# Six channel blocks summed by column additions instead of a strided reduction

## The chip, the cores and the metric

The kernel runs on one core of a Trainium2 chip. The metric is the device time of one execution in microseconds; before the change three timed runs gave 3150.18, 3155.59 and 3156.21 us, a median of 3155.59. Engines are named as the profile names them: PE is TensorE (matmuls), DVE is VectorE, ACT is ScalarE, POOL is GpSimd, SP is the queue that issues most DMAs. TensorE writes its results to the accumulator memory PSUM; the tiles that the other engines work on lie in SBUF, or are read from PSUM.

## The reference, cut to what matters

One layer of a decoder over a prompt of 2048 rows and 32 sample rows. Its input projection feeds three branches: windowed attention (A), a depthwise convolution with a LayerNorm over 768 channels (B), and cross-attention into 256 memory tokens (C). The change lies in the LayerNorm of branch B:

```
def _layernorm(x, g, b):
    x32 = x.astype(jnp.float32)
    mu = jnp.mean(x32, axis=-1, keepdims=True)
    var = jnp.mean(jnp.square(x32 - mu), axis=-1, keepdims=True)
    y = (x32 - mu) * lax.rsqrt(var + EPS)
    return (y * g.astype(jnp.float32) + b.astype(jnp.float32)).astype(x.dtype)
...
    ob = jax.nn.silu(_layernorm(conv, ln_g, ln_b))
```

## The kernel before, in words

The kernel has three large parts. The first (to about 870 us) projects the input onto q, k, v, the convolution's input and qc, and runs the convolution. The second runs the norm of branch B, the memory keys and values, the cross-attention, the sample attention and then the prompt's attention, and beside all of it a filler: the projections of the gates (tiles `gg`, function `sweep`), 7680 matmuls of 256 or 288 columns whose results ScalarE and VectorE evacuate (L243, L245, L246). The third (from about 2560 us) projects and merges the branches.

Nobody writes the order of the instructions by hand. The program is recorded, and a scheduler simulates it and fixes from its own costs and from priorities the order in which each engine's queue holds its instructions. On the chip each queue then runs strictly in that order. So TensorE has filler to do at nearly every moment, but a matmul of the norm that stands next in its queue stops it until its input is there.

The convolution's result is kept as six blocks of 128 channels by 2080 positions. `conv_norm` takes it in chunks of 256 positions (nine, the last of 32), as a tile `c` of 128 partitions by 6 blocks by 256 columns. For each chunk:

- a load brings `c` (L663); three such tiles are in use in turn;
- L665 sums the six blocks column by column into `sm`, with one `tensor_reduce` over a view in which the six values of a column are 256 elements apart;
- L667 multiplies by a matrix of ones, which sums over the partitions as well (result `str`), and L668 subtracts the mean from `c`;
- L671, on ScalarE, squares `c` into `sq`, of which there is one buffer; L673 sums its six blocks, again with a strided `tensor_reduce`; L675 is the matmul by ones (result `sco`);
- L677 makes the variance, then `rsqrt` (L63 on ScalarE, L64 to L68 on VectorE) its reciprocal root, and L679 scales `c`;
- L681, on GpSimd, applies gain and shift, one instruction a block; L684, on ScalarE, takes a tanh into the same `sq`, and L685 multiplies `c` by it. L686 stores it.

Because of the single `sq`, a chunk's square waits for L685 of the chunk before. `conv_norm` is a generator: `memory_kv` advances it by a chunk after each block of the memory projection, and `memory` runs what is left. GpSimd splits the weights meanwhile into a rounded part and a rest (L55, L56, tiles `whi` and `wlo`), for the filler and for the memory projection (matmuls `kv`).

Of the kernel before, what the change touches and what calls it, by code (L numbers as in the profile page):

```python
# [7 lines left out]
F32 = mybir.dt.float32  # L8
R32 = mybir.dt.float32r
AF = mybir.ActivationFunctionType  # L10
ALU = mybir.AluOpType
AX = mybir.AxisListType
# [25 lines left out]
class K:  # L38
# [616 lines left out]
    def conv_norm(self, lp, ps):  # L655
        nc = self.nc
        ones = lp.tile([128, 128], F32, name="ones")
        nc.vector.memset(ones, 1.0)
        W = 256
        for s in range(0, T, W):  # L660
            n = min(W, T - s)
            x = lp.tile([128, 6, W], F32, name="c", bufs=3)[:, :, :n]
            nc.sync.dma_start(x, self.d_c[:, :, s:s + n].rearrange("j p n -> p j n"))  # L663
            sm = lp.tile([128, W], F32, name="sm", bufs=2)[:, :n]
            nc.vector.tensor_reduce(sm, x.rearrange("p j n -> p n j"), axis=AX.X, op=ALU.add)  # L665
            p = ps.tile([128, 512], F32, name="str")[:, :n]
            nc.tensor.matmul(p, ones, sm, start=True, stop=True)  # L667
            nc.vector.scalar_tensor_tensor(x, p[:, None, :].to_broadcast([128, 6, n]), -1.0 / EB, x,  # L668
                                           op0=ALU.mult, op1=ALU.add)
            sq = lp.tile([128, 6, W], F32, name="sq", bufs=1)[:, :, :n]  # L670
            nc.scalar.activation(sq, x, AF.Square)  # L671
            sm = lp.tile([128, W], F32, name="sm", bufs=2)[:, :n]
            nc.vector.tensor_reduce(sm, sq.rearrange("p j n -> p n j"), axis=AX.X, op=ALU.add)  # L673
            p = ps.tile([128, 512], F32, name="sco")[:, :n]
            nc.tensor.matmul(p, ones, sm, start=True, stop=True)  # L675
            var = lp.tile([128, W], F32, name="var")[:, :n]
            nc.vector.tensor_scalar(var, p, 1.0 / EB, EPS, op0=ALU.mult, op1=ALU.add)  # L677
            rs = self.rsqrt(lp, var, [128, W], "ln", n)
            nc.vector.tensor_tensor(x, x, rs[:, None, :].to_broadcast([128, 6, n]), op=ALU.mult)  # L679
            for j in range(6):  # L680
                nc.gpsimd.tensor_scalar(x[:, j], x[:, j], self.v("ln_g", j), self.v("ln_b", j),  # L681
                                        op0=ALU.mult, op1=ALU.add)
            t = lp.tile([128, 6, W], F32, name="sq", bufs=1)[:, :, :n]
            nc.scalar.activation(t, x, AF.Tanh, scale=0.5)  # L684
            nc.vector.scalar_tensor_tensor(x, t, 1.0, x, op0=ALU.add, op1=ALU.mult)  # L685
            nc.sync.dma_start(self.d_actb[:, :, s:s + n].rearrange("j p n -> p j n"), x)  # L686
            yield
# [620 lines left out]
```

## Time and profile before

| | |
|---|---|
| Median of three timed runs | 3155.59 us |
| Profiled execution | 3154.4 us |
| Its span, first to last instruction | 3152.6 us |
| Busy in the span | PE 95%, DVE 64%, POOL 43%, ACT 36% |
| Mean granted TensorE clock | 0.979 of full speed |
| Chain that ended last | PE 70%, DMA 12%, DVE 7%, issue 4%, POOL 3%, ACT 2% |
| L665, all nine | 23.2 us of DVE |
| L673, all nine | 23.5 us of DVE |

A row of instructions reads: line, engine, operation, output<-inputs, shapes, count, then busy time. "Idle before" is how long the engine stood still in front of such instructions, and the name behind the arrow is what ended that. TensorE is busy for most of the span in every part, so the question for any stretch is how long it stands still there, and for whom.

### The profile page before, as it was taken

How to read it: one execution, taken by the hardware profiler on the slowest of the kernel's cores; microseconds unless marked ns; L12 is line 12 of the kernel's file. 1: busy time of each engine (PE TensorE's matmuls, PEld its weight loads, DVE VectorE, ACT ScalarE, POOL GpSimd, SP SyncE). 2: the span in 40 equal slices, each digit the busy share in tenths (PEclk: the TensorE clock that was granted, in tenths of full speed). 3: DMA queues.
4: the chain of work that ended last, by engine and by line, in shares of the span. 5: the costliest groups of instructions: out<-in, count | busy, mean ns of one | idle time of the engine just before them, and what ended most of it. 6: DMA issues, size and time to landing. Idle time of an engine off the chain costs nothing.

```text
span 3152.6 us, 55374 instructions
## 1 busy us (share of the span) xinstructions
PE 3000.2 (95%) x20705; PEld 2839.9 (90%) x20705; DVE 2014.8 (64%) x3734; ACT 1124.2 (36%) x2835; POOL 1350.4 (43%) x1048
## 2 busy tenths in 40 slices
PE   7999999999987999999999999989899979999998
PEld 6899999999987999998999999989898967787897
DVE  5297797796677926465546766666656457556563
ACT  5010010010132433243437575656565523222221
POOL 0121221142356537444256565667676433233240
PEclk9899999999999999999999999999999989999999
DMA  7232222211265454477454656576555487657561
GB/s 250 85 103 80 80 60 61 63 62 50 81 182 167 135 153 144 147 219 239 151 139 116 161 123 163 128 185 150 156 143 152 109 279 227 223 168 227 161 197 53
DMA packets 532218, 454.66 MB, mean 144 GB/s; under 512 B 118191, under 2 KB 458581, under 8 KB 531137
## 3 DMA queue, kind: packets, MB, share of 16 engines
q1 hardware_dynamic: 357502, 335.36, 36.2%
q10 hardware_dynamic: 169840, 105.02, 11.7%
q0 software_dynamic: 4608, 10.75, 1.2%
q8 instruction: 164, 2.69, 0.4%
q14 instruction: 104, 0.85, 0.1%
HBM read 332.96 MB, written 118.04 MB: 143 GB/s over the span
## 4 chain that ended last, share of the span: by engine, by line
PE 70%; DMA 12%; DVE 7%; issue 4%; POOL 3%; ACT 2%; SPq 1%; ACTq 0%; DVEq 0%; POOLq 0%
PE g L166 8%; PE g L167 8%; PE g L168 8%; PE gg L166 6%; PE gg L168 6%; PE gg L167 6%; PE pg L168 3%; PE pg L166 3%; PE pg L167 3%; PE pt L571 2%; DMA cb<-d_cf 2%; PE y L1180 2%; PE y L1179 2%; PE y L1178 2%; PE o L598 1%
## 5 line engine op out<-in xcount | busy, mean ns | idle before, releaser
L166 PE MATMUL gg<-x0h,whi 128*128 128x256 f32 (+1 forms) x2560 | 747.9, 292 | 25.9 <-DVE st L246 12.2
L168 PE MATMUL gg<-x0h,wlo 128*128 128x256 f32 (+1 forms) x2560 | 741.8, 290 | 0.1
L167 PE MATMUL gg<-x0l,whi 128*128 128x256 f32 (+1 forms) x2560 | 741.1, 290 | 0.0
L55 POOL TENSOR_SCALAR whi<-wraw 128x1024 fp32r<-128x1024 f32 x162 | 242.7, 1500 | 928.5 <-PE g L167 524.1
L166 PEld LDWEIGHTS gg<-x0h,whi 128*128 128x128 f32 x2560 | 493.2, 193 | 35.0 <-DVE st L246 13.7
L167 PEld LDWEIGHTS gg<-x0l,whi 128*128 128x128 f32 x2560 | 493.5, 193 | 2.2 <-issue 0.5
L168 PEld LDWEIGHTS gg<-x0h,wlo 128*128 128x128 f32 x2560 | 493.2, 193 | 2.2 <-POOL wlo L56 0.3
L322 DVE SCALAR_TENSOR_TENSOR acc<-G,cw,acc 128x1536 f32<-128x1536 f32 (+15 forms) x354 | 480.8, 1408 | 0.3
L56 POOL TENSOR_TENSOR wlo<-wraw,whi 128x1024 fp32r<-128x1024 f32 x162 | 417.0, 2575 | 9.4 <-PE gg L168 0.2
L155 POOL TENSOR_TENSOR clo<-craw,chi 128x768 fp32r<-128x768 f32 (+1 forms) x96 | 174.1, 1815 | 346.0 <-ACT chi L154 329.8
L627 ACT ACTIVATE P<-T,stm 128x128 f32<-128x128 f32 (+1 forms) x576 | 260.8, 455 | 141.0 <-DVE stm L625 94.8
L239 ACT ACTIVATE st<-g 128x384 f32<-128x384 f32 (+1 forms) x132 | 60.2, 461 | 570.7 <-PE g L168 550.7
L166 PE MATMUL pg<-ac,chi 128*128 128x512 f32 (+1 forms) x640 | 229.4, 359 | 16.6 <-ACT chi L154 8.7
L625 DVE CUSTOM_DVE_ANT_0 T<-s,bias 128x128 f32<-128x128 f32 (+1 forms) x576 | 191.5, 357 | 80.8 <-PE s L617 47.0
L167 PE MATMUL pg<-ac,chi 128*128 128x512 f32 (+1 forms) x640 | 228.8, 358 | 6.3 <-DVE ac L1198 6.3
L168 PE MATMUL pg<-ac,clo 128*128 128x512 f32 (+1 forms) x640 | 227.6, 357 | 3.6 <-POOL clo L155 3.6
L576 DVE TENSOR_TENSOR pl<-pt,ph 128x512 fp32r<-128x512 f32 x240 | 155.6, 652 | 52.4 <-ACT ph L575 48.9
L168 PE MATMUL g<-x0h,wlo 128*128 128x384 f32 x544 | 184.3, 339 | 2.9 <-POOL wlo L56 2.9
L166 PE MATMUL g<-x0h,whi 128*128 128x384 f32 x544 | 183.6, 338 | 2.6 <-ACT st L239 2.3
L167 PE MATMUL g<-x1l,whi 128*128 128x384 f32 x544 | 186.0, 342 | 0.0
L167 PE MATMUL g<-x0l,whi 128*128 128x384 f32 x544 | 185.8, 342 | 0.0
L168 PE MATMUL g<-x1h,wlo 128*128 128x384 f32 x544 | 185.8, 342 | 0.0
(330 smaller groups left out, 7425.0 us busy)
## 6 DMA issues: line engine op xcount, KB each, us to landing
wraw<-in_w_in ACTq DMA_DIRECT2D x119, 512.0 KB
d_g<-st ACTq DMA_DIRECT2D x168, 128.0 KB
cb<-d_cf SPq DMA_DIRECT2D x72, 256.0 KB
g<-d_g SPq DMA_DIRECT2D x72, 256.0 KB
wraw<-in_w_in SPq DMA_DIRECT2D x35, 512.0 KB
kvc<-in_cache_k_win SPq DMA_DIRECT2D x8, 1536.0 KB
kvc<-in_cache_v_win SPq DMA_DIRECT2D x8, 1536.0 KB
raw<-d_q SPq DMA_DIRECT2D x48, 256.0 KB
```

The costliest lines, as they stand in the source:

```text
L55: nc.gpsimd.tensor_scalar(hi, raw, 1.0, 1.0, op0=ALU.mult, op1=ALU.mult)
L56: nc.gpsimd.tensor_sub(lo, raw, hi.bitcast(F32))
L155: nc.gpsimd.tensor_sub(lo, raw, hi.bitcast(F32))
L166: nc.tensor.matmul(ps, hi[:, k, :], h, start=k == 0, stop=False)
L167: nc.tensor.matmul(ps, hi[:, k, :], l, start=False, stop=False)
L168: nc.tensor.matmul(ps, lo[:, k, :], h, start=False, stop=k == kb - 1)
L322: nc.vector.scalar_tensor_tensor(a3[:, lo:hi], G[:, src:src + hi - lo, 2 - m:130 - m], w, a3[:, lo:hi], op0=ALU.mult, op1=ALU.add)
L571: nc.tensor.transpose(t[:, 128 * x:128 * x + 128], pc, self.ident)
L576: nc.vector.tensor_tensor(pl[:, :w], t[:, :w], ph[:, :w].bitcast(F32), op=ALU.subtract)
L625: nc.vector.tensor_tensor_reduce(sc[:, :w], t[:, o:o + w], bias[:, 256 - w:256], 1.0, 3.0e38, ALU.add, ALU.min, m)
L627: nc.scalar.activation(P[:, o:o + w], sc[:, :w], AF.Exp, bias=m, scale=-1.0, accum_out=self.stl[:, col:col + 1])
L1178: nc.tensor.matmul(y[:m, c, :], ah[:, ts_], bh[:, cs], start=k == 0, stop=False)
```

## The change

Both strided reductions become chains of additions over whole blocks, whose columns lie next to each other. The first sum is five additions of 256 columns. The second is one addition of the upper three blocks onto the lower three (768 columns) and two of 256 columns; it is made in place, in `sq`, and the second `sm` tile is gone. The lines behind it move down: L667 and L668 become L669 and L670, L675 becomes L678, and from L677 on each line is three further (L677 is L680, L679 is L682, L681 is L684, L685 is L688).

```diff
-            nc.vector.tensor_reduce(sm, x.rearrange("p j n -> p n j"), axis=AX.X, op=ALU.add)
+            nc.vector.tensor_add(sm, x[:, 0], x[:, 1])
+            for j in range(2, 6):
+                nc.vector.tensor_add(sm, sm, x[:, j])
             p = ps.tile([128, 512], F32, name="str")[:, :n]
             nc.tensor.matmul(p, ones, sm, start=True, stop=True)
             nc.vector.scalar_tensor_tensor(x, p[:, None, :].to_broadcast([128, 6, n]), -1.0 / EB, x,
                                            op0=ALU.mult, op1=ALU.add)
             sq = lp.tile([128, 6, W], F32, name="sq", bufs=1)[:, :, :n]
             nc.scalar.activation(sq, x, AF.Square)
-            sm = lp.tile([128, W], F32, name="sm", bufs=2)[:, :n]
-            nc.vector.tensor_reduce(sm, sq.rearrange("p j n -> p n j"), axis=AX.X, op=ALU.add)
+            nc.vector.tensor_add(sq[:, 0:3], sq[:, 0:3], sq[:, 3:6])
+            nc.vector.tensor_add(sq[:, 0], sq[:, 0], sq[:, 1])
+            nc.vector.tensor_add(sq[:, 0], sq[:, 0], sq[:, 2])
             p = ps.tile([128, 512], F32, name="sco")[:, :n]
-            nc.tensor.matmul(p, ones, sm, start=True, stop=True)
+            nc.tensor.matmul(p, ones, sq[:, 0], start=True, stop=True)
```

The scheduler orders the norm's stretch anew on all engines. On TensorE, the rows around the second chunk's second matmul (`sco`, L675) before, with the third chunk's first matmul (`str`, L667) behind it:

```order
L166 MATMUL gg<-x0h_192,whi 128x256
L675 MATMUL sco<-sm,ones 128x256
L167 MATMUL gg<-x0l_200,whi 128x256
L168 MATMUL gg<-x0h_192,wlo 128x256
L166 MATMUL gg<-x0h_193,whi 128x256
L167 MATMUL gg<-x0l_201,whi 128x256
L168 MATMUL gg<-x0h_193,wlo 128x256
L667 MATMUL str<-sm,ones 128x256
```

Only five filler matmuls lie between the two. After the change, the same place (the matmul is L678 now):

```order
L166 MATMUL gg<-x0h_189,whi 128x256
L678 MATMUL sco<-sq,ones 128x256
L167 MATMUL gg<-x0l_197,whi 128x256
L167 MATMUL kv<-ml,whi 128x256
L168 MATMUL kv<-mh,wlo 128x256
L167 MATMUL kv<-ml,whi 128x256
L168 MATMUL kv<-mh,wlo 128x256
L168 MATMUL gg<-x0h_189,wlo 128x256
```

The next `str` (now of the fourth chunk, the third's having moved ahead) comes 127 matmuls behind this `sco`. In the whole norm an `sco` is followed by the next `str` after 1 to 15 matmuls before and after 25 to 127 now, while from one `sco` to the next it is still about 210.

On VectorE, the rows behind the second chunk's product L685 before; `mrow` is a copy for the memory branch, `st<-st,gg` an evacuation of the filler:

```order
L685 SCALAR_TENSOR_TENSOR c<-sq,c 128x1536
L673 TENSOR_REDUCE sm<-sq 128x256
L665 TENSOR_REDUCE sm<-c 128x256
L246 SCALAR_TENSOR_TENSOR st<-st,gg 128x256
L945 COPY mrow<-tr 128x256
L677 TENSOR_SCALAR var<-sco 128x256
```

The third chunk's second sum is followed at once by the fourth's first sum, and then by the third's variance. After the change, behind the same product (now L688):

```order
L688 SCALAR_TENSOR_TENSOR c<-sq,c 128x1536
L948 COPY mrow<-tr 128x256
L246 SCALAR_TENSOR_TENSOR st<-st,gg 128x256
L674 TENSOR_TENSOR sq<-sq 128x768
L246 SCALAR_TENSOR_TENSOR st<-st,gg 128x256
L675 TENSOR_TENSOR sq<-sq 128x256
L676 TENSOR_TENSOR sq<-sq 128x256
L246 SCALAR_TENSOR_TENSOR st<-st,gg 128x256
L680 TENSOR_SCALAR var<-sco 128x256
L64 RECIPROCAL lnr<-lns 128x256
L665 TENSOR_TENSOR sm<-c 128x256
L65 TENSOR_TENSOR lns<-lnr 128x256
```

The next first sum (L665, and its L667 further on) has moved behind the variance, and its additions alternate with the steps of the reciprocal root.

At the start of the norm VectorE held, before, the first sum, the centering and then two evacuations of the filler:

```order
L665 TENSOR_REDUCE sm<-c 128x256
L668 SCALAR_TENSOR_TENSOR c<-str,c 128x1536
L246 SCALAR_TENSOR_TENSOR st<-st,gg 128x256 x2
L673 TENSOR_REDUCE sm<-sq 128x256
L665 TENSOR_REDUCE sm<-c 128x256
```

Now it holds there:

```order
L665 TENSOR_TENSOR sm<-c 128x256
L667 TENSOR_TENSOR sm<-sm,c 128x256 x4
L665 TENSOR_TENSOR sm<-c 128x256
L667 TENSOR_TENSOR sm<-sm,c 128x256 x4
L670 SCALAR_TENSOR_TENSOR c<-str,c 128x1536
L665 TENSOR_TENSOR sm<-c 128x256
L246 SCALAR_TENSOR_TENSOR st<-st,gg 128x256 x2
```

The second chunk's first sum and the beginning of the third's have moved ahead of the two evacuations.

## Rows read from the trace of the kernel before

**Rows 1.** Windows: engines' busy us (instructions), granted clock, DMA share, GB/s.

```profile
870.00:1133.00 263.00, 226.24 (x1746) 218.28 (x1745) 206.47 (x270) 98.28 (x182) 152.59 (x140) 0.95 0.53 162
880.00:900.00 20.00, 11.43 (x51) 9.86 (x50) 16.19 (x17) 7.62 (x11) 13.46 (x8) 0.67 0.60 173
940.00:960.00 20.00, 9.89 (x65) 8.82 (x64) 18.45 (x9) 3.45 (x6) 16.23 (x14) 0.79 0.46 136
980.00:1000.00 20.00, 15.68 (x112) 14.83 (x110) 17.34 (x11) 5.78 (x8) 7.70 (x7) 0.91 0.40 126
1140.00:1300.00 160.00, 160.00 (x1284) 154.39 (x1284) 68.76 (x164) 55.26 (x155) 83.40 (x71) 1.00 0.43 132
```

**Rows 2.** Waits of TensorE, 865 to 1140 us: us in total, times, longest.

```profile
PE sco L675 <- DVE sm L673: 14.9, 5, 9.0
PE gg L166 <- DVE st L246: 10.1, 9, 1.8
PE str L667 <- DVE sm L665: 4.5, 5, 1.4
PE gg L166 <- POOL whi L55: 3.9, 1, 3.9
PE str L667 <- DVE mss L917: 1.5, 1, 1.5
```

**Rows 3.** Groups of VectorE, 865 to 1135 us: busy us, mean ns | idle before.

```profile
L685 DVE SCALAR_TENSOR_TENSOR c<-sq,c 128x1536 f32<-128x1536 f32 x8 | 35.0, 4372 | 19.3 <-ACT sq L684 19.3
L673 DVE TENSOR_REDUCE sm<-sq 128x256 f32<-128x1536 f32 x8 | 23.0, 2876 | 9.5 <-ACT sq L671 9.5
L665 DVE TENSOR_REDUCE sm<-c 128x256 f32<-128x1536 f32 x8 | 22.7, 2840 | 0.7 <-DMA c<-d_c 0.7
L679 DVE TENSOR_TENSOR c<-c,lnr 128x1536 f32<-128x1536 f32 x8 | 14.0, 1753 | 0.1
...
L65 DVE TENSOR_TENSOR lns<-lnr 128x256 f32<-128x256 f32 x8 | 6.3, 785 | 0.0
L66 DVE TENSOR_TENSOR lns<-lns,var 128x256 f32<-128x256 f32 x8 | 5.1, 643 | 0.1
...
L68 DVE TENSOR_TENSOR lnr<-lns,lnr 128x256 f32<-128x256 f32 x8 | 3.4, 421 | 0.1
```

**Rows 4.** Timeline of TensorE: start us, us, instruction [idle before <-releaser].

```profile
919.74 0.70 PE L667 MATMUL str<-sm,ones 128*128 128x256 f32 x2 [1.40 <-DVE sm L665]
...
955.50 1.22 PE L675 MATMUL sco<-sm,ones 128*128 128x256 f32 x2 [9.04 <-DVE sm L673]
```

**Rows 5.** Timeline of VectorE, the same columns.

```profile
883.39 2.84 DVE L673 TENSOR_REDUCE sm<-sq 128x256 f32<-128x1536 f32 x1 [5.98 <-ACT sq L671]
...
938.52 12.59 DVE L685 SCALAR_TENSOR_TENSOR c<-sq,c 128x1536 f32<-128x1536 f32 x1 [2.60 <-ACT sq L684]
...
952.66 2.79 DVE L673 TENSOR_REDUCE sm<-sq 128x256 f32<-128x1536 f32 x1 [1.55 <-ACT sq L671]
955.37 2.79 DVE L665 TENSOR_REDUCE sm<-c 128x256 f32<-128x1536 f32 x1
...
958.74 0.41 DVE L677 TENSOR_SCALAR var<-sco 128x256 f32<-128x256 f32 x1
```

**Rows 6.** Timeline of GpSimd, the same columns.

```profile
883.12 1.04 POOL L55 TENSOR_SCALAR whi<-wraw 128x1024 fp32r<-128x1024 f32 x1 [33.79 <-DMA wraw<-in_w_in]
...
936.92 2.41 POOL L56 TENSOR_TENSOR wlo<-wraw,whi 128x1024 fp32r<-128x1024 f32 x1
...
948.46 1.04 POOL L55 TENSOR_SCALAR whi<-wraw 128x1024 fp32r<-128x1024 f32 x1
```

**Rows 7.** Group of GpSimd, 865 to 1135 us: busy us, mean ns | idle before.

```profile
L56 POOL TENSOR_TENSOR wlo<-wraw,whi 128x1024 fp32r<-128x1024 f32 x26 | 63.4, 2445 | 0.9
```

## The prediction, made before the changed kernel ran

> **What bounds the kernel now.** I read the windows first, then the waits of TensorE, then the groups of VectorE, then timelines. The norm works between 870 and 1133 us. In that stretch TensorE is busy 226.24 of 263 us, so it idles 36.8 us; from 1140 to 1300 us it idles not at all [rows 1]. Its queue is in order and always has filler matmuls (gg) to do, so time that TensorE loses in the norm's stretch isn't made up behind it: what the change is worth is how much of the 36.8 us goes. The waits say who causes them [rows 2]: 14.9 us in five waits of the second matmul (sco) for the second sum, 4.5 us in five waits of the first matmul (str) for the first sum, 1.5 us more at a str behind VectorE's memory norm, and 10.1 us of filler behind evacuations on VectorE. So 20.9 us stand at the two matmuls behind the two sums. One of the five sco waits is 9.0 us long, the other four are 5.9 us together.
>
> The long one shows the second thing to see. At 938.52 VectorE starts L685, which multiplies two SBUF tiles and normally takes about what L679 takes, 1.75 us; it takes 12.59 us [rows 3, 5]. GpSimd has instructions back to back from 936.92 until 949.50 (948.46 + 1.04) [rows 6], and L685 ends 1.6 us behind their end. The strided sums of two chunks that follow, at 952.66 and 955.37, take 2.79 us each [rows 5], as in every other place (mean 2.88 and 2.84 [rows 3]), whatever GpSimd does. VectorE instructions that read two SBUF tiles are held by GpSimd, the strided sums are not.
>
> **The change part by part.** *Removed:* eight strided sums at 2.840 us and eight at 2.876 us, 45.7 us of VectorE [rows 3]; the ninth chunk has 32 columns and is left out of the sum.
>
> *Added:* five additions of 256 columns for each first sum, and for each second sum one of 768 columns and two of 256. A free 256-column instruction with two SBUF tiles takes 0.421 us (L68). For 768 columns no row exists; between L68 and L679 (1536 columns, 1.753 us) the slope is 1.04 ns a column, so 0.421 + 512 x 0.00104 = 0.95 us [rows 3]. The first sum becomes 2.11 us, the second 1.80 us, both 31.2 us in all: VectorE does 14.5 us less if nothing holds it.
>
> *Moved.* TensorE's order shows sco and the next chunk's str 6 matmuls apart before; afterwards no str follows for 127. So the first sum need no longer be ready at once behind the second. VectorE's order agrees: before, L665 stands between the second sum and L677, which takes up sco's result; afterwards the next first sum stands behind that instruction, and its additions are laid between the steps of the reciprocal root. I take the str waits as gone: 4.5 + 1.5 = 6.0 us, less the 1.40 us at 919.74 [rows 4], which lies in the same round as the 9.04 us wait and is counted there: 4.6 us.
>
> For sco, the chain from one sco to the next shortens by two pieces. The second sum loses 2.88 - 1.80 = 1.08 us. And L677 starts at 958.74, though the matmul of 955.50 was over at 956.72 [rows 4, 5]: L665 was in the way for 2.0 us. Together 3.1 us a chunk. The four short waits (5.9 us, the chain is shorter by more than each) go, and 3.1 us of the long one: 9.0 us. So 13.6 us without any hold.
>
> *The price.* All 64 full additions read two SBUF tiles, and so can be held by GpSimd. From below, the nearest rows by shape are L65, L66 and L68: means 0.785, 0.643 and 0.421 us, so 0.20 us above free on average [rows 3]. From above there is L685: 4.372 against 1.753, 2.6 us above free for each [rows 3]. The additions of the first sums stand among L65 to L68, and TensorE comes for them 76 to 127 matmuls after the sco before (25 for the short last chunk); I charge TensorE nothing for them (8.0 us on VectorE by 0.20 each, less than the 14.5 us given back). The second sum follows the square on ScalarE and TensorE comes for it soon. L673 began while GpSimd was busy in five chunks of eight; the first is 883.39 within GpSimd's 883.12 to 884.16 [rows 5, 6]. A wait from a random moment of a 2.445 us instruction of GpSimd (wlo, 26 of them here [rows 7]) is 1.2 us on average, so 0.76 us for the 768-column addition, and 0.20 for each of the two others: 1.16 us a chunk. In the five chunks where TensorE waits at sco that is 5.8 us. I take this value, nearer to the rows with the same shape, and keep 0 and 2.6 us an instruction for the range.
>
> The Trainium skill (SBUF — State Buffer, § Who interferes with whom) says that a VectorE instruction with two SBUF inputs contends with a GpSimd instruction that reads SBUF, and that `tensor_reduce` on trn2 never contends. The rows on L685 and on the strided sums agree with both. By that rule the change takes the one kind of sum that can't be held and puts in the kind that can; the rival below gives it its time.
>
> *The start.* Before, VectorE evacuated two filler tiles right behind the first centering; now the additions of the second and third chunk stand ahead, and wait for their loads. TensorE had 3.9 us of waiting for a weight split there anyway [rows 2]; I charge nothing, and if that cover is short it is at most these 4 us. The loads themselves keep their places on SP's queue but for one row. On GpSimd's queue the scaling of the second chunk now stands behind three more splits and one rounding, some 5 us of work; these same instructions held L685 until 949.50 before, so I charge nothing. The granted clock falls behind long waits, to 0.67, 0.79 and 0.91 of full speed (between the levels of 1.2 and 2.4 GHz) [rows 1]; the share lost there, (0.33 x 11.4) + (0.21 x 9.9) + (0.09 x 15.7) = 7.3 us, may come back in part. I count none of it. From the first sample-attention matmul on the order on TensorE is the same as before, but for single rows, until late in the prompt attention, so what is gained is carried along; the changed last part I take as nothing, by 5 us either way.
>
> *Sum:* -4.6 - 9.0 + 5.8 = -7.8 us. Against the profiled execution (3154.4 us, of which 3152.6 us span) that is 3146.6 us. The median of the three timed runs is 3155.6, 1.2 us above the profiled one, so on that scale 3147.8 us.
>
> **The rivals.** *GpSimd holds the second sums (slower).* Place: L674 to L676, behind the square. If each of the three is held h us, a chunk's chain changes by 3h - 3.1, in five chunks, and the 4.6 us of str waits are still gained: 5 x (3h - 3.1) - 4.6. With h the whole of one wlo, 2.445 us, this is +16.6 us, 3172 us. It is no loss until h is 1.34 us and a loss that can be measured from 1.76 us on. For it: GpSimd is busy 152.6 of the 263 us [rows 1], and L685, which stands at just such a place behind a ScalarE step, loses 2.6 us on average. Against it: half of that is one event of 12.59 us, and L68 and L679 are not held at all. [...]
>
> *The waits form again (no change).* The last thing on the chain at 951 us was L685, not a sum; if TensorE arrives earlier it may wait there longer. With h near 1.3, or with half of the 13.6 us given back, the time is 3152 to 3156 us. For it: 10.1 us of the idle time hang on evacuations, which the change only shuffles [rows 2]. Against it: the five chunks' chain really has fewer microseconds.
>
> *More goes than I count (much faster).* If nothing is held and the clock stays up, 13.6 + 7.3 = 20.9 us: 3134.7 us. For it: the low clock stands right behind these waits. Against it: the 880 to 900 us stretch also waits for weights.
>
> **How the numbers follow.** The forecast (3147.8) gets 0.39, the larger gain 0.06, no change 0.33, the hold 0.22. 0.2% is 6.3 us, about what a measurement of this kernel tells from no change. So faster by over that 0.45, within it 0.33, slower 0.22. The forecast's own range is 3141 to 3149. The whole range is 3136 to 3165: it leaves out the extreme end of the larger gain and the hold beyond about 2 us an instruction.
>
> **What would show it.** Right: no L665 or L673 group of 2.8 us but additions of 0.42 to 0.6 us; TensorE's waits for the first sum gone, those for the second under 10 us; TensorE's idle time in the norm's stretch down from 36.8 to about 29 us, and the end earlier by that. Wrong: a 768-column addition of 2 us or more on average and 256-column ones of more than 1 us, with TensorE waiting for them (the hold); or additions at their free price and TensorE's idle time where it was, behind L688 or the evacuations (waits that form again); or a gain in the stretch that a later one takes back.

## The result and the profile after

The changed kernel takes 3164.17 us (median of seven executions, 3157.49 to 3170.2), the kernel before 3152.62 us beside it (seven, 3145.42 to 3156.21). The ratio is 1.0041, with a 95% interval of 1.0024 to 1.0058: about 11.5 us slower, where 7.8 us faster was forecast. The forecast's own range (3141 to 3149 us) does not hold the time, the whole range (3136 to 3165 us) just does; the direction is wrong.

The profiled execution after took 3164.17 us, its span is 3162.4 us (before 3152.6). Two points that both kernels pass with the same matmuls behind them but for single ones cut the span into stages: the first str matmul and the first score matmul of the sample attention (tile S). The timeline of TensorE, after (start us, us, instruction, [idle before <-releaser]):

```profile
871.45 0.59 PE L669 MATMUL str<-sm,ones 128*128 128x256 f32 x2
...
1344.74 0.77 PE L807 MATMUL S<-KTh,qz 128*112 128x512 f32 x1 [3.29 <-ACT KTh L797]
```

and of the kernel before:

```profile
874.28 0.67 PE L667 MATMUL str<-sm,ones 128*128 128x256 f32 x2
...
1338.83 0.48 PE L804 MATMUL S<-KTh,qz 128*112 128x512 f32 x1 [2.77 <-ACT KTh L794]
```

From one to the other it is 464.6 us before and 473.3 us after: 8.7 us more. The changed kernel came to the first point 2.8 us earlier, and behind the second it needs 3.9 us more; that makes the 9.8 us between the spans. So the loss lies mostly where the change is. The same stretch in windows (busy us and instructions of PE, PE's weight loads, DVE, ACT, POOL; granted clock; DMA share; GB/s), after:

```profile
867.00:1150.00 283.00, 243.31 (x1839) 235.78 (x1838) 208.41 (x324) 103.52 (x189) 161.26 (x142) 0.93 0.50 155
```

and before, an equal length from an equal start:

```profile
870.00:1153.00 283.00, 246.24 (x1900) 237.50 (x1898) 206.47 (x270) 102.35 (x190) 159.43 (x144) 0.95 0.52 159
```

TensorE idles 39.7 us instead of 36.8, the granted clock of the stretch is 0.93 instead of 0.95, and 61 fewer matmuls are recorded. At the 160.00 us for 1284 matmuls of the stretch without idle time [rows 1] these 61 are 7.6 us. Of those, 2.9 us are the longer idle time; the other 4.7 us go into matmuls that take longer on average, at the lower granted clock. VectorE is not busy for less time (208.41 us, before 206.47), though 14.5 us should have come off it. Where TensorE waits now, 865 to 1150 us (us in total, times, longest), to be read against [rows 2]:

```profile
PE gg L166 <- DVE st L246: 27.0, 12, 8.4
PE str L669 <- DVE c L670: 3.7, 1, 3.7
PE str L669 <- DVE mrr L64: 3.6, 1, 3.6
...
PE str L669 <- DVE sm L667: 1.4, 1, 1.4
...
PE sco L678 <- DVE sq L676: 0.2, 1, 0.2
```

The waits at sco fell from 14.9 to 0.2 us. Those at str rose from 6.0 to 8.7. Those of the filler for evacuations on VectorE rose from 10.1 to 27.0 us. The groups of VectorE show why (busy us, mean ns | idle before), against [rows 3]:

```profile
L667 DVE TENSOR_TENSOR sm<-sm,c 128x256 f32<-128x256 f32 x32 | 19.0, 594 | 0.3
L688 DVE SCALAR_TENSOR_TENSOR c<-sq,c 128x1536 f32<-128x1536 f32 x8 | 17.6, 2200 | 13.6 <-ACT sq L687 13.6
...
L674 DVE TENSOR_TENSOR sq<-sq 128x768 f32<-128x768 f32 x8 | 12.9, 1616 | 3.5 <-ACT sq L673 3.5
L713 DVE COPY sb<-sn 112x32 f32<-112x32 f32 x3 | 9.7, 3222 | 6.5 <-DMA sn<-d_exs 6.5
L665 DVE TENSOR_TENSOR sm<-c 128x256 f32<-128x256 f32 x8 | 7.7, 959 | 2.8 <-DMA c<-d_c 2.8
...
L675 DVE TENSOR_TENSOR sq<-sq 128x256 f32<-128x256 f32 x8 | 5.6, 696 | 0.0
...
L676 DVE TENSOR_TENSOR sq<-sq 128x256 f32<-128x256 f32 x8 | 3.4, 428 | 0.1
```

The additions take 19.0 + 7.7 + 12.9 + 5.6 + 3.4 = 48.6 us, the strided sums took 45.7 [rows 3]. Without holds they would be 31.2 us, so 17.4 us are holds. The long event of the kernel before moved: GpSimd's burst, which held the last pass of a chunk for 12.59 us [rows 5, 6], now holds a copy of 32 columns. VectorE's timeline, after:

```profile
922.94 2.55 DVE L665 TENSOR_TENSOR sm<-c 128x256 f32<-128x256 f32 x1 [0.18 <-DMA c<-d_c]
925.41 2.56 DVE L65 TENSOR_TENSOR lns<-lnr 128x256 f32<-128x256 f32 x1
927.89 0.41 DVE L246 SCALAR_TENSOR_TENSOR st<-st,gg 128x256 f32<-128x256 f32 x1
...
940.02 9.06 DVE L713 COPY sb<-sn 112x32 f32<-112x32 f32 x1 [5.96 <-DMA sn<-d_exs]
```

GpSimd's:

```profile
922.84 2.37 POOL L56 TENSOR_TENSOR wlo<-wraw,whi 128x1024 fp32r<-128x1024 f32 x1
...
925.17 2.52 POOL L56 TENSOR_TENSOR wlo<-wraw,whi 128x1024 fp32r<-128x1024 f32 x1
...
937.87 1.05 POOL L55 TENSOR_SCALAR whi<-wraw 128x1024 fp32r<-128x1024 f32 x1
938.88 2.39 POOL L56 TENSOR_TENSOR wlo<-wraw,whi 128x1024 fp32r<-128x1024 f32 x1
...
948.32 0.73 POOL L56 TENSOR_TENSOR kl<-kt,kh 128x256 fp32r<-128x256 f32 x1
```

and TensorE's:

```profile
875.75 0.70 PE L669 MATMUL str<-sm,ones 128*128 128x256 f32 x2 [3.71 <-DVE c L670]
885.11 1.19 PE L669 MATMUL str<-sm,ones 128*128 128x256 f32 x2 [3.62 <-DVE mrr L64]
928.35 0.58 PE L166 MATMUL gg<-x0h,whi 128*128 128x256 f32 x1 [3.98 <-DVE st L246]
953.45 0.58 PE L166 MATMUL gg<-x0h,whi 128*128 128x256 f32 x1 [8.41 <-DVE st L246]
```

At 922.94 an addition of the first sum and the next instruction are held, each through one of GpSimd's two subtractions; the evacuation (L246) behind them starts at 927.89, and TensorE has waited 3.98 us for it. At 940.02 the copy has waited 5.96 us for its load, and then stays until 949.08, just behind the end of GpSimd's last instruction (948.32 + 0.73 = 949.05). Two long passes, two copies and the evacuation stand behind it; TensorE waits 8.41 us. At 875.75 the second str waits 3.71 us until the first centering has read the one PSUM tile of this name: the first sums, drawn ahead, are done early but their matmul can't start.

### The profile page after: what moved, and what is told of

Read it like the earlier page. It is cut to its first block, busy times and chain, and to the rows that moved or that the text cites. A ratio compares the mean times of both kernels' runs of the same rounds, so it can differ in the third digit from the quotient of the medians.

```text
span 3162.4 us, 55447 instructions
## 1 busy us (share of the span) xinstructions
PE 3004.0 (95%) x20705; PEld 2845.2 (90%) x20705; DVE 2018.9 (64%) x3788; ACT 1126.7 (36%) x2837; POOL 1356.8 (43%) x1048
## 4 chain that ended last, share of the span: by engine, by line
PE 70%; DMA 13%; DVE 7%; issue 4%; POOL 3%; SPq 1%; ACT 1%; ACTq 0%; DVEq 0%; POOLq 0%
PE g L166 8%; PE g L167 8%; PE g L168 8%; PE gg L166 6%; PE gg L167 6%; PE gg L168 6%; PE pg L168 3%; PE pg L166 3%; PE pg L167 3%; DMA cb<-d_cf 3%; PE pt L571 2%; PE o L598 2%; PE s L617 2%; PE s L616 2%; PE y L1182 1%
## 5 line engine op out<-in xcount | busy, mean ns | idle before, releaser
L166 PEld LDWEIGHTS gg<-x0h,whi 128*128 128x128 f32 x2560 | 496.8, 194 | 48.6 <-DVE st L246 33.0
L166 PE MATMUL pg<-ac,chi 128*128 128x512 f32 (+1 forms) x640 | 229.1, 359 | 19.1 <-ACT chi L154 10.1
```

Source lines behind the costliest of these rows:

```text
L166: nc.tensor.matmul(ps, hi[:, k, :], h, start=k == 0, stop=False)
```

## The experiments

Two theories. *Holds:* the additions have both inputs in SBUF, VectorE waits with them while GpSimd works, and what stands behind them comes late. *Order:* with other instructions the scheduler makes another order (first sums drawn ahead, the third bias copy in front of two passes), and that costs the time, not the additions.

**The hold by itself.** The program repeats these instructions, separated by barriers:

```
add : tensor_add(sm, x[:, 0], x[:, j])          wide: tensor_add of 768 columns
sum : tensor_reduce over six blocks             acc : tensor_add(u_in_psum, u_in_psum, x[:, j])
copy: tensor_copy to 112x32        GpSimd: tensor_sub(lo, raw, hi), or rounding, of 128x1024
```

> A small program that computes none of the reference: VectorE runs additions of 256 and 768 columns, strided sums of six blocks, additions with one input in PSUM, and small copies, each first with GpSimd idle and then beside a burst of four or eight of GpSimd's 128x1024 subtractions or roundings. Theory of the holds: with GpSimd idle an addition takes 0.42 us and a wide one 0.96 us; beside the subtractions the 16 additions, 6.7 us of work, last 11 us or more, and single ones take over 1.5 us; the strided sum stays at 2.8 us, the addition into PSUM at its free time, and the subtraction itself takes 2.4 us alone and at most 2.9 us beside additions. Theory of the order: the long additions of the trace were long for another reason (a late input that the records count as busy), so additions here stay under 0.5 us beside GpSimd.

VectorE, first with GpSimd idle (first four rows), then beside GpSimd:

```profile
13.68 0.42 DVE L109 TENSOR_TENSOR sm<-x 128x256 f32<-128x256 f32 x1
14.02 0.95 DVE L113 TENSOR_TENSOR big<-x 128x768 f32<-128x768 f32 x1
14.88 2.73 DVE L117 TENSOR_REDUCE sm<-x 128x256 f32<-128x1536 f32 x1
...
28.86 0.18 DVE L125 COPY cp<-x 112x32 f32<-112x32 f32 x1
...
48.94 2.44 DVE L109 TENSOR_TENSOR sm<-x 128x256 f32<-128x256 f32 x1
51.42 2.44 DVE L109 TENSOR_TENSOR sm<-x 128x256 f32<-128x256 f32 x1
...
59.31 0.42 DVE L109 TENSOR_TENSOR sm<-x 128x256 f32<-128x256 f32 x1
...
64.46 1.14 DVE L109 TENSOR_TENSOR sm<-x 128x256 f32<-128x256 f32 x1
...
78.10 2.98 DVE L113 TENSOR_TENSOR big<-x 128x768 f32<-128x768 f32 x1
...
93.15 2.79 DVE L117 TENSOR_REDUCE sm<-x 128x256 f32<-128x1536 f32 x1
...
104.43 0.43 DVE L121 TENSOR_TENSOR u<-u,x 128x256 f32<-128x256 f32 x1
...
114.44 2.27 DVE L125 COPY cp<-x 112x32 f32<-112x32 f32 x1
```

GpSimd at the first two held additions:

```profile
48.59 2.51 POOL L129 TENSOR_TENSOR lo<-raw,hi 128x1024 f32<-128x1024 f32 x1 [0.19 <-SPq L140]
51.18 2.40 POOL L129 TENSOR_TENSOR lo<-raw,hi 128x1024 f32<-128x1024 f32 x1
```

One addition gets through per GpSimd instruction: 2.44 us beside the subtraction, 1.14 us beside the shorter rounding, 0.42 us again once GpSimd is done (59.31). The wide one takes 2.98 us. The strided sum (2.79 against 2.73) and the addition into PSUM (0.43) are not held. The small copy is, at 2.27 us. Holds was right, on the copy it had said nothing. The Trainium skill (SBUF — State Buffer, § Who interferes with whom) states that two SBUF inputs on VectorE contend with a GpSimd instruction that reads SBUF, that copies can contend too, and that a `tensor_reduce` on trn2 never does; the rows agree with all three.

**Less work on GpSimd, for both kinds of sum.** Both kernels with this edit:

```
+ hi = rounding of raw on GpSimd; return hi, hi    # lo = raw - hi left out
```

> The kernel before without the low halves of the weights of the gate blocks and the memory's keys and values: GpSimd's subtraction of 2.4 us per block is left out, and the third product reads the high half instead, so that TensorE does the same work. It is the yardstick for the next run. Either theory: TensorE's waits on the weights (3.9 us) go, so 0 to 10 us faster than before, ratio 0.997 to 1.000.

> The changed kernel with the same subtractions left out. Its order on VectorE still has the first sums drawn ahead, the third bias copy behind its loads and the additions in the same places. Theory of the holds: with most of GpSimd's work gone the additions run at 0.42 and 0.96 us, their sum in the stretch falls from 48.6 us to 31 to 36 us, the waits on L246 fall from 27 us to under 15 us, and the kernel is 3 to 9 us faster than the yardstick (ratio of the two 0.997 to 0.999). Theory of the order: it stays 6 to 12 us slower than the yardstick (ratio 1.002 to 1.004), with the waits at str and at the bias copy still there.

Measured: with strided sums 0.9963 of before (0.9945 to 0.998), with additions 0.9918 (0.99 to 0.9937), so with GpSimd's subtraction gone the additions are 11.0 us faster than the strided sums (3121.93 against 3132.92 us), more than the 3 to 9 expected. The scheduler ordered each of the two anew, so a part of this can be the order's. TensorE's waits for evacuations on VectorE are 3.2 us in the one with additions; its order still had first sums drawn ahead. The additions took 37.6 us in the stretch, a little more than the 31 to 36 expected: GpSimd's roundings, which hold an addition for 1.14 us in the small program, are still there.

**The additions in the old order, the strided sums in the new.** The scheduler's order differs for each edit, so six kernels had it pinned: an ordering edge, with no wait, from each instruction to the next on its engine, over the whole program.

```
+ for a, b in zip(order[engine], order[engine][1:]): add_manual_dep(b, a.name, NoSync)
```

> The additions of the changed kernel, but every engine's instructions pinned to the order of the kernel before, with a sum's additions standing together where its strided sum stood. Theory that the holds alone make the loss: it is as slow as the changed kernel, 6 to 12 us over before (1.002 to 1.004). Theory that the order alone makes it: the additions then give what their free durations promise, 3 to 9 us under before (0.997 to 0.999). If it takes both (an addition or a copy drawn to a bad place, and GpSimd's burst there), it ends between, 0.999 to 1.001.

> The strided sums of before, with every engine's instructions pinned to the order of the changed kernel; a strided sum stands where the last addition of its sum stood (the second sum's tile has buffers of its own, so that sums drawn ahead do not wait for it). Holds alone: 3 us faster to 3 us slower than before (0.999 to 1.001). Order alone: 8 to 14 us slower (1.0025 to 1.0045), with the wait of 8 us behind the third bias copy and the one at str in it.

> Sums gathered in PSUM (a copy and five additions with one input in PSUM each), every engine pinned to the order of the kernel before, the six instructions of a sum standing together where its strided sum stood. The pair of the additions with both inputs in SBUF in that same order, which came out 18 us slower than before. Theory of the holds: no addition is held, six take 2.5 us a sum, so 2 to 8 us faster than before (0.9975 to 0.9995) and some 20 to 25 us faster than the pair. Rival, the loss of the pair came from more and shorter instructions in the chain and not from holds: 6 to 15 us slower than before (1.002 to 1.005).

The last one sums into PSUM:

```
- nc.vector.tensor_reduce(sm, x ..., axis=AX.X, op=ALU.add)
+ nc.vector.tensor_copy(u, x[:, 0])              # u: columns 256 to 511 of the str tile
+ for j in range(1, 5): nc.vector.tensor_add(u, u, x[:, j])
+ nc.vector.tensor_add(sm, u, x[:, 5])           # the second sum alike, in the sco tile
```

Each ratio is to executions of the kernel before that ran beside that kernel (a median of 3149.21 us, for the PSUM sums 3149.65, for the last row 3152.62).

| sums | order | median us (executions) | ratio to before, 95% |
|---|---|---|---|
| strided (before) | old | 3149.21 (29) | 1 |
| additions, both inputs in SBUF | old | 3167.09 (6) | 1.0057, 1.0039 to 1.0075 |
| additions, one input in PSUM | old | 3148.41 (12) | 1.0004, 0.9989 to 1.002 |
| strided | new | 3157.16 (12) | 1.0026, 1.001 to 1.0043 |
| additions (the changed kernel) | new | 3164.17 (7) | 1.0041, 1.0024 to 1.0058 |

Between the first three rows nothing but the sums differs: the traces show all other instructions of TensorE, VectorE, GpSimd and SyncE in the same sequence. The additions in SBUF cost 18 us there; with one input in PSUM, though more of them, they cost nothing. The kernel before was not run with the ordering edges, but the PSUM sums have them and keep its time, so the edges are not what costs the 18 us. So the holds make a loss without any new order, larger than was expected of them. The gain that the PSUM sums were expected to show did not come either. The new order costs 8 us with strided sums by the medians; its profiled execution (3142.41 us) was the fastest of twelve, so that its trace doesn't show where. With additions the new order is not worse than the old (the intervals overlap). Those of the last two rows overlap too, so the totals alone do not tell additions from strided sums in the new order. TensorE's waits with the additions in the old order, 865 to 1150 us:

```profile
PE sco L678 <- DVE sq L676: 18.8, 6, 8.9
PE str L669 <- DVE sm L667: 13.6, 6, 5.0
PE gg L166 <- DVE st L246: 11.2, 9, 2.9
```

Here, where a sum stands close before its matmul, the holds show at sco and str [rows 2: 14.9 and 4.5]; in the changed kernel the same holds showed at the evacuations. The stage from the first str to the first S, in the profiled execution:

```profile
877.67 0.59 PE L669 MATMUL str<-sm,ones 128*128 128x256 f32 x2
...
1357.85 0.48 PE L807 MATMUL S<-KTh,qz 128*112 128x512 f32 x1 [3.20 <-ACT KTh L797]
```

These are 480.2 us, against 464.6 before and 464.4 with the PSUM sums. The same two points and TensorE's waits with the strided sums in the new order:

```profile
873.14 0.59 PE L667 MATMUL str<-sm,ones 128*128 128x256 f32 x2
...
1334.06 0.48 PE L804 MATMUL S<-KTh,qz 128*112 128x512 f32 x1 [2.78 <-ACT KTh L794]
```

```profile
PE gg L166 <- DVE st L246: 13.4, 9, 2.8
...
PE sco L675 <- DVE sm L673: 3.6, 3, 1.5
```

That stage took 460.9 us; with the additions, in the same order, it took 473.3 us and the evacuations were waited for 27.0 us. So in the profiled executions the additions lengthen the stage by 15.6 us in the old order and by 12.4 us in the new one, and the new order by itself does not lengthen it; the execution with strided sums in the new order is, as said, the fastest of its twelve. The sco waits, on the other hand, are mostly gone in the new order with strided sums too (3.6 us left). Behind the first S such readings are coarser: there the first three rows of the table, with the same sequence of instructions, took 1813.8, 1802.6 and 1804.9 us.

**GpSimd's subtraction in four pieces.** Nothing is left out:

```
- nc.gpsimd.tensor_sub(lo, raw, hi)
+ for k in range(0, 8, 2): nc.gpsimd.tensor_sub(lo[:, k:k+2], raw[:, k:k+2], hi[:, k:k+2])
```

First in the scheduler's own order, then pinned to the order of the changed kernel and of the kernel before.

> The changed kernel with GpSimd's subtraction of 1024 columns (the low half of the weights of the gate blocks and of the memory's keys and values) cut into four of 256 columns; nothing is left out, and GpSimd works some 0.5 us longer per block. Theory of the holds, with what the small program shows (one addition gets in between two of GpSimd's instructions): a held addition waits for 0.7 us at most beside these and not for 2.4 us, the additions of the stretch take 36 to 42 us and not 48.6 us, and the kernel is 8 to 16 us faster than the changed kernel, ratio to before 0.998 to 1.001. Theory of the order: no gain, ratio 1.003 to 1.006.

> The kernel before with GpSimd's subtraction cut into four of 256 columns, as the control of the changed kernel with that cut. Theory of the holds: the strided sums were never held, but other lines of VectorE with two inputs in SBUF were (the last pass of a chunk took 4.4 us and not 1.8), so this kernel gains too, but less than the changed kernel's 18 us: 2 to 8 us faster than before, ratio 0.9975 to 0.9995, and the difference between additions and strided sums shrinks from 11.5 us to 4 to 9 us. Theory of the order: the cut does nothing here (0.999 to 1.001) and the 18 us of the changed kernel came from its changed order.

> The changed kernel with GpSimd's subtraction cut into four pieces, every engine pinned to the changed kernel's own order, so that nothing differs but the pieces. Holds: the wait at a piece is 0.7 us at most and not 2.4, and the time falls by 6 to 14 us against the changed kernel, ratio to before 0.9995 to 1.002. Order alone: no gain, 1.003 to 1.006, since GpSimd works longer.

> The strided sums of before, in the order of before on every engine, with GpSimd's subtraction cut into four pieces and nothing else changed. Theory of the holds: lines other than the sums are held in the kernel before too (the last pass of a chunk took 35.0 us for eight where 14 are free, and additions in the prompt attention), so 3 to 12 us faster than before (0.996 to 0.999). Rival, the 18 us that the cut gave with the scheduler's own order were that order's: 0.999 to 1.001.

Additions: 1.0007 (0.9992 to 1.0021) in the scheduler's order and 1.0007 (0.9992 to 1.0023) pinned to the changed kernel's, so the pieces alone take back some 0.34 points of the loss, as much as the holds were expected to give back. In the pinned one the stage up to the first S took 464.9 us, 8.4 less than after. The additions themselves gained less than expected: 42.8 us in the stretch pinned and 47.1 in the scheduler's order, after 48.6, where 36 to 42 were expected. The third bias copy gained nothing: 11.57 us in the pinned one, behind a burst of pieces. Strided sums: 0.9984 (0.9969 to 0.9999) pinned, 5.6 us, where 3 to 12 were expected, but not where they were expected: the last passes of the chunks, which were to be held less, took 36.0 us and not fewer than the 35.0 before. 0.9941 (0.9925 to 0.9957), 3131.22 us, in the scheduler's order. This last is the fastest complete kernel of all, but only 5.6 of its 18 us are there with the order pinned; the rest came with its own. In the scheduler's orders the distance between additions and strided sums grew with the pieces, from 0.41 to 0.66 points, where it was expected to shrink; pinned, it is 0.23.

**The third bias copy.** Once all three copies behind the cross-attention, with both kinds of sum (the scheduler makes a new order), once this one copy seven places later in the pinned order:

```
- nc.vector.tensor_copy(bt[:, 640:NK] ...)      # in sample_bias
+ with tc.issue_after(first.ins): nc.vector.tensor_copy(bt[:, 640:NK] ...)   # in sample_attention
```

> The changed kernel with the three copies of the sample bias put behind the cross attention, out of the stretch of the normalization; nothing is left out. Theory that one event makes the loss (the bias copy, 6.0 us behind its loads and then 9.1 us behind GpSimd, with 8.4 us of TensorE's wait at 953): 7 to 9 us faster than the changed kernel, ratio to before 1.000 to 1.002. Theory of the holds: the burst of GpSimd then catches an addition instead, and only the 6 us behind the loads are won in part: 0 to 4 us faster than the changed kernel, ratio to before 1.003 to 1.005.

> The kernel before with the three copies of the sample bias put behind the cross attention, as the control of the changed kernel with that move. In the kernel before these copies took 2.8 us and TensorE waited for none of them. Theory of the holds: GpSimd's burst catches the last pass of a chunk here as it did before, so nothing or little changes: 0.9985 to 1.0005. Theory that the copies themselves cost time wherever they stand: as much won as in the changed kernel, 5 to 8 us, ratio 0.9975 to 0.9985.

> The changed kernel in its own order with one instruction of VectorE moved: the third copy of the sample bias stands seven instructions later, behind the second sum of its chunk. If that copy (6.0 us behind its loads, 9.1 us behind GpSimd) makes the loss: 6 to 9 us faster than the changed kernel, ratio to before 1.000 to 1.002. If GpSimd's burst then catches the next instruction with both inputs in SBUF (the last pass of the chunk, as in the kernel before, 12.6 us): 0 to 4 us faster, 1.003 to 1.004.

Additions with the copies late: 1.0021 (1.0007 to 1.0035), at the edge of what the one event was expected to give (1.000 to 1.002) and better than what the holds were (1.003 to 1.005); strided sums with the copies late: 1.0013 (0.9999 to 1.0026), against nothing or a gain expected. Both have new orders. The one copy moved: 1.0037 (1.0023 to 1.0051), no gain that can be told. In its profiled execution the event is gone: the pass L688 gets in ahead of GpSimd, and now GpSimd is the one that waits, 1.96 us for a rounding of 0.41.

```profile
941.03 1.75 DVE L688 SCALAR_TENSOR_TENSOR c<-sq,c 128x1536 f32<-128x1536 f32 x1
```

```profile
941.08 1.96 POOL L55 TENSOR_SCALAR kh<-kt 128x256 fp32r<-128x256 f32 x1
```

The stage up to the first S took 461.7 us there, 11.6 less than after; from the first score matmul of the prompt attention to the first y it took 1047.7 us, 8.1 more. Why that part is longer is open, and executions with the same sequence of instructions differ behind the first S by as much. By the total, the loss can't be put down to this one event.

**Half the change each, and the PSUM sums in the scheduler's order.**

```
first_only:  additions for sm from c, tensor_reduce for sm from sq
second_only: tensor_reduce for sm from c, additions in sq      (second_look: the same again)
```

> The additions for the first sum alone; the second sum strided as before. Theory of the holds: in the changed kernel the five additions of a chunk took 3.3 us (26.7 us for eight) where the strided sum took 2.8 us (22.7 us), so this half is worth a loss by itself: 3 to 9 us slower than before, ratio 1.001 to 1.003. Theory of the order: the first sums are what the scheduler draws ahead at the start, so this half alone gives nearly the whole loss, ratio 1.003 to 1.005.

> The additions for the second sum alone; the first sum strided as before. Theory of the holds: the three additions took 2.7 us a chunk (21.9 us) where the strided sum took 2.9 us (23.0 us), so VectorE gains 1 us in all and the wait at sco goes: 4 us faster to 3 us slower than before, ratio 0.9987 to 1.001. Theory of the order: some other order, 0 to 6 us slower, ratio 1.000 to 1.002, and not to be told from its mechanism by the time alone.

> The kernel with the additions for the second sum alone once more, for its profile: the first profile was of its fastest execution (3154.9 us, the others 3169 to 3181). If holds make the slow ones: an execution of 3169 us or more shows TensorE's waits on VectorE in the stretch of the normalization at 35 us or more, where the fast one had 25. If the loss lies elsewhere: the stretch up to 1150 us looks as in the fast one and the time goes after the first score product of the sample attention (1344.8 us).

> Both sums by a copy and five additions of 256 columns that gather in unused columns of the PSUM tile, so that every addition has one input in PSUM. Theory of the holds: no addition is held (0.42 us each beside GpSimd too), six take 2.5 us a chunk against 2.9 us for the strided sum, and the kernel is 2 to 8 us faster than before (0.9975 to 0.9995) and 13 to 19 us faster than the changed kernel. Theory of the order: sixteen more instructions than the changed kernel has in the same places, drawn ahead in the same way, 6 to 14 us slower than before (1.002 to 1.0045).

> Sums gathered in PSUM, and GpSimd's subtraction cut into four: a try at a version that beats both kernels by more. Theory of the holds: what is still held beside the PSUM sums (the last pass of a chunk, 31.3 us for eight where 14 us are free) gains from the cut, 3 to 9 us faster than the PSUM sums alone, ratio to before 0.994 to 0.9965. Rival, GpSimd's longer work (0.5 us more a block) makes the weights late: 0.9965 to 0.999.

The first half alone: 1.0036 (1.002 to 1.0052), above what the holds were expected to give (1.001 to 1.003) and within what the order was (1.003 to 1.005). The second half alone: 1.0077 (1.0056 to 1.0099), which neither theory had; both its profiles (3154.92 and 3157.53 us) are of executions faster than its median of 3170.01 us and show no such loss. It stays unexplained, and the halves don't add up to the whole. PSUM sums: 0.9967 (0.9949 to 0.9984), 3137.49 us, faster than both kernels, by a little more than expected (0.9975 to 0.9995); by the pinned run above this gain came with the order and not with the sums alone. PSUM sums with the pieces: 1.0074 (1.0053 to 1.0095), the opposite of what was expected. There the profile shows most of the cause, at the start of the last part:

```profile
2560.45 0.79 PE L169 MATMUL pg<-ac,chi 128*128 128x512 f32 x1 [12.41 <-ACT chi L154]
...
2602.09 0.77 PE L169 MATMUL pg<-ac,chi 128*128 128x512 f32 x1 [26.88 <-DVE mix L1163]
```

In the order of the kernel before, 301 filler matmuls stand behind the last value matmul of the prompt attention and cover the start of the projections; in this order there are none left. From 2540 to 2700 us TensorE waits 42.6 us, with the PSUM sums alone 15.6: 27.0 of the 34.6 us between the two spans. An order that uses up the filler early pays for it 1400 us later.

## Why the prediction was wrong

*What failed* is the step "I charge TensorE nothing" for the additions of the first sums. Their price on VectorE was nearly right. The second sums took 1616 + 696 + 428 ns = 2.74 us a chunk, 0.94 above the free 1.80, where 1.16 was charged; the first sums took (19.0 + 7.7) / 8 = 3.34 us, 1.23 above the free 2.11, where 1.0 was charged. By the prediction's own prices the holds are 8.0 + 8 x 1.16 = 17.3 us of VectorE, and 17.4 us were measured. But it set only the 8.0 us of the first sums against the 14.5 us that VectorE was to get back. With all of them nothing is left: VectorE loses 2.8 us by these prices and 2.9 us as measured (48.6 against 45.7).

*Where it was paid.* The prediction looked for the holds' cost only at the matmul that reads the sum. TensorE didn't come early for the first sums, and yet paid, since the evacuations stand behind them in VectorE's queue: L246 27.0 us instead of 10.1, the term of which the rival said that "the change only shuffles" it. With the strided sums in the same new order it is 13.4 us, so most of the rise goes with the additions. The pinned kernel shows the other way to pay: with the old order it is sco and str.

*What held, in part by luck.* The free durations (0.42 and 0.95 us) were right. The sco waits went, by 14.7 us and not by 9.0, but they do so with strided sums in the new order too (3.6 us left), and with the additions in the old order they rise to 18.8. So it was the order, with the first sum out of the way (2.0 of the 3.1 us a chunk), and not a shorter second sum: that came out 0.14 us shorter, not 1.08. The burst at 938 was named, but not that it would catch whatever stands next: the 9.04 us wait, from which 3.1 us were to go, became one of 8.41 us behind the copy.

*The other terms.* The str waits were to go (4.6 us); three others of 8.7 us stand there, two of them from sums drawn ahead (the one PSUM tile, 3.71, and an addition held before it, 3.62). The start was charged nothing by the cover of 3.9 us on a weight split; that wait went, and these came. The clock was to give something back, if anything; it fell from 0.95 to 0.93, and 4.7 us of the stretch's loss go with it.

*The rival* of the hold had the mechanism, but put it at the second sums alone, where it would have decided from 1.34 us an instruction. They were held by 0.31 us each. Its place, not its mechanism, was wrong, and its chance of 0.22 had been weighed for that place.

*What stays open.* The new order by itself costs something (1.0026 with strided sums) whose place no trace shows; it also made the str waits at the start (3.71 and 3.62 us; 4.2 and 4.5 with strided sums). One edit, the pieces with strided sums, gave 0.9941 in the scheduler's order and 0.9984 in the pinned one; another, the PSUM sums, 0.9967 and 1.0004. Where the pieces help the strided sums is open as well. So the total of a single edit that reorders can't be read to better than some 0.4%.

## What to carry to other kernels

Price an instruction with both inputs in SBUF by what GpSimd does at that moment, up to one whole GpSimd instruction each and now and then a whole burst, add these prices up over all such instructions, and look for the cost at everything queued behind it, evacuations first. A slower instruction that is never held, or additions with one input in PSUM, can be the better choice beside a busy GpSimd; shorter pieces on GpSimd helped here too, by 0.16 to 0.34 points with the order pinned, though not by all that they were expected to free. Where a scheduler reorders the program on every edit, pin the order and change one thing before believing a reason for a few tenths of a per cent.

## What was not expected of the hardware

An addition beside GpSimd did not slow down by some share but ran in lockstep: one per GpSimd instruction, 2.44 us beside a subtraction and 1.14 us beside a rounding. In the small program a gap of 0.08 us stands between GpSimd's instructions (48.59 + 2.51 to 51.18) and the addition gets through there. In the kernel's burst each instruction starts before the last has ended (937.87 + 1.05 against 938.88), and the copy waited through eight of them for 9.06 us. The missing gap can't be the whole reason: at 925.17 a subtraction of GpSimd also starts before the one at 922.84 has ended (925.21), and the addition of 922.94 got through there. Why the copy, and the pass of 12.59 us before it, stayed for a whole burst is open. The hold goes both ways: GpSimd's 0.41 us rounding took 1.96 us behind a pass that had started first.
